# SSD output and z with channels on partitions, roots through memory, half the gate's adaLN moved

## The chip, the cores and the metric

The kernel runs on one core of a Trainium2 chip. The metric is the device time of one execution in microseconds, here the median of three runs. The engines are TensorE (PE, its weight loads PEld), VectorE (DVE), ScalarE (ACT), GpSimd (POOL) and the sync engine (SP), which issues nearly all the DMAs, in program order.

## The reference, cut to what matters

A trunk of two layers on one sequence of L = 256 steps and D = 2048 channels, float32. Layer A is a Mamba-2 SSD mixer, layer B a dilated attention. Each layer gets shift, scale and gate from a conditioning vector c (adaLN), and ends in a residual sum and a LayerNorm. The change lies in layer A:

```python
z, xBC, dt = split(h @ in_w)                 # z: 4096, xs: 4096, B and C: 1024 each, 64 heads
xBC = silu(causal_conv(xBC));  xs, B, C = split(xBC)
dt = softplus(dt + dt_bias);   acum = cumsum(dt * -exp(A_log))
# per group g of 8 (8 heads of 64 channels, one B and C of 128 states), s <= l
y[l] = sum_s (C[l]·B[s]) * exp(acum[l] - acum[s]) * dt[s] * xs[s]   + D_skip * xs[l]
y = y * silu(z)
y = y * rsqrt(mean(y^2 over the group's 512 channels) + eps) * norm_g
out = y @ out_w                              # 4096 -> 2048
x = layer_norm(alpha * x + (1 + gate) * out)
```

## The kernel before, in words

**Products.** Every float32 operand of a large product is split into a high and a low part, and three products are summed: high by high, high by low, low by high. Weights arrive in pieces of 512 KB (`load_piece`, L90, six `raw` buffers); ScalarE makes the high half (`whi`, L100), VectorE the low half (`wlo`, L102), with four buffers of each, so weights can be prepared up to four pieces ahead. A product has one of three forms. `cm_piece` (L151 to 153) holds the weights in TensorE and moves 256 time steps: 24 matmuls of 256 columns a piece, and the result has channels on partitions. `tm_piece` (L232 to 234, in the order of L224 where `low_last` is set) holds the activations and moves 512 weight columns: 12 matmuls of 512 a piece, with time on partitions. `cm_wide` (L190, L193) is a variant of the first.

**Stages.** In the start stage the adaLN dots of shift and scale (L317, one VectorE instruction of 2048 elements for each 128 outputs) make h, while the first pieces of several products run by a table, `order`; 27 of the 64 pieces of z lie here. Then comes a loop over the groups: `product` makes B and C, xs or z of the next group; `scores` (L743) makes C·B; `stage1` (L754) loads the cumulated decays of four heads onto all partitions (`cbc`, L760, two buffers), makes the decay matrix `seg` with Relu and Exp on ScalarE, transposes xs (L776) into `xd`; `stage2` (L793) makes the part of the first half of the sequence (`po`, L798) and the diagonal parts (`py`, L809), adds, multiplies by silu(z), squares (L812) and takes the root (`rsqrt`, L275 to 281, on VectorE); `stage3` (L817) scales y by it on ScalarE (L820), with time on partitions. The last z product (group 7) has the last group's stage1 beside it.

**Out.** `y_tiles` (L857) transposes y (L864) to channels on partitions, multiplies by the norm's weight and splits it: high on ScalarE (L868), low on VectorE (L869). Group 0 is done in the last z product; `y_ahead` does groups 1 to 7 in the first of four out products (n = 0 to 3, `tm_chunk` over `wout[n]`, 16 pieces of two 128-channel tiles each, 512 of the 2048 output channels). Beside n=0 run the second half of the gate's dots (eight), then `gate_out` (a transpose, a copy at L330, a write to `gated`); after each n the gate is broadcast from there and `residual` (L904, L905) is made. V and K, attention and its own out product follow, and are untouched.

**Order.** Each engine runs its instructions in an order that the tile framework's planner sets from the program; `issue_after` pins single ones behind others, and `background(*rate)` takes one job (such as a dot) from a queue every so many pieces.

## Time and profile before

| | us |
|---|---|
| median of three runs (1224.0 to 1226.15) | 1224.74 |
| the profiled execution's own time | 1223.81 |
| its span in the trace, at a clock of 0.999 | 1222.0 |
| TensorE busy | 1208.8 |
| VectorE busy | 1019.6 |
| ScalarE busy | 703.9 |
| start stage and first product, about | 0 to 200 |
| loop over groups, about | 200 to 479 |
| last z product, group 7 | 482.3 to 507.9 |
| first out product, n=0 | 507.9 to 561.4 |

Times in the trace count from the span's first instruction; the profiled execution's own time is 1.8 us longer than the span. In a row of the timeline stand the start, the time it took, the engine, the line, the operation, output and input tiles and their sizes, how many in a row, and in brackets the idle time ahead with what ended it. In a group's row the last columns are busy time in us, mean ns of one, and idle time ahead. A matmul's shown length includes its way through the array, so its price is the distance from its start to the next one's. A float32 matmul of two float32 operands leaves two records.

### The profile page before, as it was taken

How to read it: one execution, taken by the hardware profiler on the slowest of the kernel's cores; microseconds unless marked ns; L12 is line 12 of the kernel's file. 1: busy time of each engine (PE TensorE's matmuls, PEld its weight loads, DVE VectorE, ACT ScalarE, POOL GpSimd, SP SyncE). 2: the span in 40 equal slices, each digit the busy share in tenths (PEclk: the TensorE clock that was granted, in tenths of full speed). 3: DMA queues.
4: the chain of work that ended last, by engine and by line, in shares of the span. 5: the costliest groups of instructions: out<-in, count | busy, mean ns of one | idle time of the engine just before them, and what ended most of it. 6: DMA issues, size and time to landing. Idle time of an engine off the chain costs nothing.

```text
span 1222.0 us, 19072 instructions
## 1 busy us (share of the span) xinstructions
PE 1208.8 (99%) x7244; PEld 1039.5 (85%) x7244; DVE 1019.6 (83%) x1450; ACT 703.9 (58%) x1057; POOL 3.9 (0%) x8
## 2 busy tenths in 40 slices
PE   8999999999999999999999999999999999999998
PEld 8889998898888888788888888888888888888886
DVE  6989997899988999899778588888987885756886
ACT  4554567787698898764335455444435844444751
POOL 0000000000000000000000000000000000000001
PEclk9999999999999999999999999999999999999999
DMA  9999976796765556689998668989997875365673
GB/s 374 421 421 423 422 264 239 259 327 224 230 190 194 182 173 207 226 327 334 370 317 298 211 203 342 350 344 379 385 376 280 281 261 174 113 193 160 193 260 69
DMA packets 81372, 335.94 MB, mean 275 GB/s; under 512 B 9200, under 2 KB 9984, under 8 KB 68480
## 3 DMA queue, kind: packets, MB, share of 16 engines
q1 hardware_dynamic: 80496, 333.59, 75.6%
q0 software_dynamic: 576, 1.05, 0.6%
q8 instruction: 57, 0.93, 0.3%
q14 instruction: 35, 0.29, 0.1%
q10 hardware_dynamic: 208, 0.08, 0.0%
HBM read 331.45 MB, written 3.23 MB: 274 GB/s over the span
## 4 chain that ended last, share of the span: by engine, by line
PE 77%; DVE 13%; ACT 5%; DMA 3%; issue 2%; DVEq 0%; ACTq 0%
PE acc L224 25%; PE acc L190 21%; PE acc L193 11%; DVE wlo L102 4%; DVE araw L317 4%; PE acc L233 3%; PE acc L234 3%; PE acc L232 3%; DMA raw<-in_win 3%; ACT whi L100 2%; DVE cacc L391 2%; PE acc L151 1%; PE acc L153 1%; PE acc L152 1%; PE py L809 1%
## 5 line engine op out<-in xcount | busy, mean ns | idle before, releaser
L100 ACT ACTIVATE whi<-raw 128x1024 fp32r<-128x1024 f32 x389 | 408.2, 1057 | 329.5 <-PE acc L190 107.1
L102 DVE TENSOR_TENSOR wlo<-raw,whi 128x1024 fp32r<-128x1024 f32 x389 | 470.2, 1221 | 128.3 <-ACT whi L100 121.1
L190 PE MATMUL acc<-actT,whi 128*128 128x512 f32 x1280 | 401.7, 394 | 0.5 <-DVE xs L202 0.5
L193 PEld LDWEIGHTS acc<-actT,wlo 128*128 128x128 f32 x1280 | 239.6, 188 | 52.3 <-DVE wlo L102 0.7
L193 PE MATMUL acc<-actT,wlo 128*128 128x256 f32 x1280 | 255.2, 281 | 0.3 <-DVE wlo L102 0.3
L317 DVE SCALAR_TENSOR_TENSOR araw<-araw,cb__72 128x2048 f32<-128x2048 f32 x95 | 217.0, 2284 | 3.2 <-DMA araw<-in_ada 3.0
L190 PEld LDWEIGHTS acc<-actT,whi 128*128 128x128 f32 x1280 | 195.0, 188 | 1.7 <-DVE xs L202 0.9
L224 PE MATMUL acc<-whi,actT 128*128 128x512 f32 x560 | 144.5, 392 | 0.5 <-ACT whi L100 0.5
L224 PEld LDWEIGHTS acc<-whi,actT 128*128 128x128 f32 x560 | 104.2, 188 | 22.0 <-ACT whi L100 0.9
L233 PE MATMUL acc<-wlo,actT 128*128 128x512 f32 x272 | 106.8, 393 | 2.2 <-DVE wlo L102 2.1
L232 PE MATMUL acc<-whi,actT 128*128 128x512 f32 x272 | 105.0, 394 | 0.2 <-ACT sz L664 0.2
L151 PE MATMUL acc<-actT,whi 128*128 128x256 f32 x372 | 103.5, 281 | 1.0 <-ACT sz L664 0.5
L224 PE MATMUL acc<-wlo,actT 128*128 128x512 f32 x384 | 103.6, 391 | 0.0
L153 PE MATMUL acc<-actT,wlo 128*128 128x256 f32 x372 | 101.9, 281 | 1.5 <-DVE wlo L102 1.5
L152 PE MATMUL acc<-actT,whi 128*128 128x256 f32 x372 | 103.0, 279 | 0.0
L234 PE MATMUL acc<-whi,actT 128*128 128x512 f32 x256 | 100.0, 391 | 0.0
L224 PEld LDWEIGHTS acc<-wlo,actT 128*128 128x128 f32 x384 | 71.7, 188 | 14.4
L151 PEld LDWEIGHTS acc<-actT,whi 128*128 128x128 f32 x372 | 69.6, 188 | 2.6 <-ACT sz L664 0.9
L153 PEld LDWEIGHTS acc<-actT,wlo 128*128 128x128 f32 x372 | 68.9, 188 | 2.3 <-DVE wlo L102 2.3
L152 PEld LDWEIGHTS acc<-actT,whi 128*128 128x128 f32 x372 | 70.6, 190 | 0.2
L233 PEld LDWEIGHTS acc<-wlo,actT 128*128 128x128 f32 x272 | 51.1, 188 | 13.8 <-DVE wlo L102 3.7
L232 PEld LDWEIGHTS acc<-whi,actT 128*128 128x128 f32 x272 | 50.9, 188 | 10.5 <-ACT sz L664 0.6
(324 smaller groups left out, 1293.5 us busy)
## 6 DMA issues: line engine op xcount, KB each, us to landing
araw<-in_ada SPq DMA_DIRECT2D x96, 1024.0 KB, 7.3
raw<-in_win SPq DMA_DIRECT2D x109, 512.0 KB, 6.0
raw<-in_wout SPq DMA_DIRECT2D x64, 512.0 KB, 5.7
raw<-in_wbin SPq DMA_DIRECT2D x64, 512.0 KB, 4.1
raw<-in_wxs SPq DMA_DIRECT2D x48, 512.0 KB, 4.5
raw<-in_wv SPq DMA_DIRECT2D x48, 512.0 KB, 6.7
raw<-in_wk SPq DMA_DIRECT2D x48, 512.0 KB, 7.6
cbc<-cumd SPq DMA_DIRECT2D x16, 512.0 KB, 5.1
```

The costliest lines, as they stand in the source:

```text
L100: copied.append(S.activation(hi, raw, AF.Copy))
L102: latest.append(V.tensor_tensor(lo, raw, hi.bitcast(F32), op=ALU.subtract))
L151: T.matmul(o, hi[:, k, c_], ahi[:, kt, :], start=first, stop=False, skip_group_check=True)
L152: T.matmul(o, hi[:, k, c_], alo[:, kt, :], start=False, stop=False, skip_group_check=True)
L153: T.matmul(o, lo[:, k, c_], ahi[:, kt, :], start=False, stop=kt == k1 - 1, skip_group_check=True)
L190: T.matmul(ps[n], hi[:, k, n * P:n * P + P], both(kt), start=kt == 0, stop=False, skip_group_check=True)
L193: T.matmul(ps[n][:, 0, :], lo[:, k, n * P:n * P + P], high(kt), start=False, stop=kt == KT - 1, skip_group_check=True)
L224: T.matmul(ps[b], a_(kt)[:, b * P:b * P + P], w_[:, k, :], start=a_ is ahi and w_ is hi and kt == k0, stop=w_ is lo and kt == k1 - 1)
L232: T.matmul(o, h_, hi[:, k, :], start=kt == k0, stop=False, skip_group_check=part)
L233: T.matmul(o, h_, lo[:, k, :], start=False, stop=False, skip_group_check=part)
L234: end = T.matmul(o, l_, hi[:, k, :], start=False, stop=kt == k1 - 1, skip_group_check=part)
L317: return V.scalar_tensor_tensor(raw, raw, 1.0, cb_, op0=ALU.mult, op1=ALU.mult, accum_out=mod[layer][:, ct, j:j + 1])
```

## The change

Everything between `stage1` and the out product now has channels on partitions. z is made by `cm_quad` (pieces of 24 matmuls of 256 instead of 12 of 512), in the start stage too, so tiles of y and z are [128, 4, 256] instead of [128, 2, 512]. `po` is four matmuls of 128 columns instead of one of 512; `py` is 16 matmuls of 128 columns a group instead of 32 of 64, alternating between the two halves of the output's partitions. The decay factor of `po` is Exp of `cbc`, made in place (`grow`), so `cbc` is read until stage2's product. The D-skip term goes from VectorE to ScalarE. The squares are made in one ScalarE instruction, added over the four channel tiles by two VectorE adds, and over partitions by two matmuls with a column of ones. `stage3` takes the root on VectorE and writes it to memory (`rootd`, GpSimd's queue); `y_tiles` reads it back broadcast over the partitions (sync queue: group 0, groups 1 to 4, groups 5 to 7) and multiplies by norm weight and root in one VectorE instruction a channel tile (L871 in the changed kernel), then splits with one 1024-element instruction on ScalarE (L875) and one on VectorE (L876). The 64 transposes of L864 are gone. `stage3` of group 7 moves into n=0. The second half of the gate's dots goes at one per three pieces over n=0 and n=1, and `gate_out` with the residual of n=0 is made at piece 12 of n=1. Line numbers in the changed kernel differ a little: L760 becomes L752, L224 L228, L317 L320.

The diff, cut to its core:

```diff
-    def cm_quad(src, ahi, alo, rate=(0, 1), k0=0):
+    def cm_quad(src, ahi, alo, rate=(0, 1), k0=0, pre=None):
         ps = acc_pair()
         for q in range(k0 // 2, KT // 2):
+            if pre:
+                pre(q)
             w = first_or(src, q, SHORT)
             if q == KT // 2 - 1:
                 begin_next()
-            cm_piece(src, q, ps, ahi, alo, k0=k0, w=w)
+            end = cm_piece(src, q, ps, ahi, alo, k0=k0, w=w)
             background(*rate)
+        z_end[:] = [end]
...
-        y = [slots.tile([P, 2, 512], F32, name=f"s{g}") for g in range(G)]
+        y = [slots.tile([P, 4, L], F32, name=f"s{g}") for g in range(G)]
...
+        rootd = dr.tile([G * L], F32, name="rootd", bufs=1)
...
+                ps = cm_quad(src, hhi, hlo, rate=R, k0=k0, pre=pre)
                 if kind == "z":
-                    ps = tm_chunk(src, hh_, hl_, rate=R, k0=k0, pre=pre, low_last=False)
                     if g not in sz:
-                        sz[g] = p0.tile([P, 2, 512], F32, name="sz")
+                        sz[g] = p0.tile([P, 4, L], F32, name="sz")
                     with behind_next():
-                        for b in range(2):
+                        for w in range(2):
+                            c_ = slice(2 * w, 2 * w + 2)
                             if part is not None:
-                                V.tensor_tensor(part[:, b, :], ps[b], part[:, b, :], op=ALU.add)
-                            S.activation(sz[g][:, b, :], part[:, b, :] if part is not None else ps[b], AF.Silu)
+                                V.tensor_tensor(part[:, c_, :], ps[w], part[:, c_, :], op=ALU.add)
+                            S.activation(sz[g][:, c_, :], part[:, c_, :] if part is not None else ps[w], AF.Silu)
                     return
...
+                    for n, rows_ in enumerate((slice(0, 64), slice(64, 128))):
+                        S.activation(cbc[rows_, 0:4:2, 0, :], cbc[rows_, n:4:2, 1, :], AF.Exp)
+                    grow.append(cbc[:, 0:4:2, 0, :])
...
-                    V.tensor_tensor(y[g][:, b, :].rearrange("p (h e) -> p h e", h=HPG), heads,
-                                    dskip[:, g * HPG:(g + 1) * HPG, None].to_broadcast([P, HPG, 64]),
-                                    op=ALU.mult)
...
+                for i in range(4):
+                    S.activation(y[g][:, i, :], xs[g][:, i, :], AF.Copy, scale=pv("dsk")[:, 4 * g + i:4 * g + i + 1])
+                return segs, xd, cb, xo, grow
+
+            def stage2(g, segs, xd, cb, xo, grow):
...
                 po = aux.tile([P, 512], F32, name="aux")
-                T.matmul(po, cb[:, 2, :], xo, start=True, stop=True)
-                V.tensor_tensor(xo.rearrange("p (h e) -> p h e", h=HPG), po.rearrange("p (h e) -> p h e", h=HPG),
-                                dec[:, 1, g * HPG:(g + 1) * HPG, None].to_broadcast([P, HPG, 64]), op=ALU.mult)
-                V.tensor_tensor(y[g][:, 1, :], xo, y[g][:, 1, :], op=ALU.add)
-                behind = z_end[-1] if g in (0, 4, 7) else None
+                behind = z_end[-1] if g in (0,3,4,7) else None
+                for i in range(4):
+                    c_ = slice(i * P, i * P + P)
+                    with tc.issue_after(behind.ins) if behind is not None else ExitStack():
+                        behind = T.matmul(po[:, c_], xo[:, c_], cb[:, 2, :], start=True, stop=True)
+                xo = xo.rearrange("p (i n) -> p i n", i=4)
+                for w in range(2):
+                    c_ = slice(2 * w, 2 * w + 2)
+                    V.tensor_tensor(xo[:, c_, :], po.rearrange("p (i n) -> p i n", i=4)[:, c_, :], grow[w], op=ALU.mult)
+                V.tensor_tensor(y[g][:, :, P:], xo, y[g][:, :, P:], op=ALU.add)
+                for w in range(2):
+                    py = aux2.tile([P, 2, L], F32, name="py")
+                    for b in range(2):
+                        for hh in range(4):
+                            h = 4 * w + hh
+                            t_ = slice(64 * (hh % 2), 64 * (hh % 2) + 64)
+                            with tc.issue_after(behind.ins):
+                                behind = T.matmul(py[t_, hh // 2, b * P:b * P + P], xd[:, b, 64 * h:64 * h + 64],
+                                         segs[w][:, hh, b, :], start=True, stop=True)
+                    c_ = slice(2 * w, 2 * w + 2)
+                    V.tensor_tensor(y[g][:, c_, :], py, y[g][:, c_, :], op=ALU.add)
+                V.tensor_tensor(y[g], y[g], sz[g], op=ALU.mult)
+                sq = sz[g]
+                S.activation(sq, y[g], AF.Square)
+                V.tensor_tensor(sq[:, 0:2, :], sq[:, 0:2, :], sq[:, 2:4, :], op=ALU.add)
+                V.tensor_tensor(sq[:, 0, :], sq[:, 0, :], sq[:, 1, :], op=ALU.add)
+                return sq[:, 0, :]
+
+            def stage3(g, sums):
+
+                ss = (aux if g == G - 1 else aux2).tile([P, 512], F32, name="aux" if g == G - 1 else "py")[:, :2]
                 for b in range(2):
-                    py = aux2.tile([P, 512], F32, name="py")
-                    for hh in range(HPG):
-                        e_ = slice(64 * hh, 64 * hh + 64)
-                        for t_ in (slice(0, 64), slice(64, 128)):
-                            with tc.issue_after(behind.ins) if behind is not None else ExitStack():
-                                T.matmul(py[t_, e_], segs[hh // 4][:, hh % 4, b, t_], xd[:, b, e_], start=True, stop=True)
-                    V.tensor_tensor(y[g][:, b, :], py, y[g][:, b, :], op=ALU.add)
-                    V.tensor_tensor(y[g][:, b, :], y[g][:, b, :], sz[g][:, b, :], op=ALU.mult)
-                    S.activation(py, y[g][:, b, :], AF.Square, accum_out=ss[:, b:b + 1])
+                    T.matmul(ss[:, b:b + 1], sums[:, b * P:b * P + P], ones[:, 0:1], start=True, stop=True)
                 ms = sm.tile([P, 2], F32, name="ms")
                 V.tensor_scalar(ms, ss, 1.0 / 512, EPS, op0=ALU.mult, op1=ALU.add)
-                return rsqrt(ms, "a")
-
-            def stage3(g, rs):
-
-                for b in range(2):
-                    S.activation(y[g][:, b, :], y[g][:, b, :], AF.Copy, scale=rs[:, b:b + 1])
+                nc.gpsimd.dma_start(rootd[g * L:g * L + L].rearrange("(b p) -> p b", p=P), rsqrt(ms, "a"))
...
+                if g == 0:
+                    roots[0] = p0.tile([P, L], F32, name="cacc", bufs=3)
+                    bcast(roots[0], rootd)
+                elif g in (1, 5):
+                    t = slots.tile([P, 4, L], F32, name=f"s{g // 5}")
+                    roots.update({g + j: t[:, j, :] for j in range(min(4, G - g))})
+                    bcast(t.rearrange("p i l -> p (i l)")[:, :min(4, G - g) * L], rootd, g * L)
+                rb = roots[g]
                 for i in range(4):
-                    ct = 4 * g + i
-                    if i % 2 == 0:
-                        pt = aux.tile([P, 512], F32, name="aux").rearrange("p (i l) -> p i l", i=2)
-                    for b in range(2):
-                        T.transpose(pt[:, i % 2, b * P:b * P + P], y[g][:, b, i * P:i * P + P], ident)
-                    w = pv("normg")[:, ct:ct + 1]
-                    hi, lo = (t.rearrange("p (r j) -> p r j", r=2) for t in y_to(ct))
-                    by_parity = pt[:, i % 2, :].rearrange("p (j r) -> p r j", r=2)
-                    S.activation(hi, by_parity, AF.Copy, scale=w)
-                    V.scalar_tensor_tensor(lo, by_parity, w, hi.bitcast(F32), op0=ALU.mult, op1=ALU.subtract)
-
+                    V.scalar_tensor_tensor(y[g][:, i, :], y[g][:, i, :], pv("normg")[:, 4 * g + i:4 * g + i + 1], rb,
+                                           op0=ALU.mult, op1=ALU.mult)
+                val = y[g].rearrange("p i (j r) -> p i r j", r=2)
+                hi, lo = (t.rearrange("p i (r j) -> p i r j", r=2) for t in y_to(g))
+                S.activation(hi, val, AF.Copy)
+                V.tensor_tensor(lo, val, hi.bitcast(F32), op=ALU.subtract)
+
+            y_first, roots = [], {}
+
+            def y_to(g):
+                return y_first if g == 0 else (yhi[g // 4][:, 4 * g % 16:4 * g % 16 + 4, :], ylo[g])
...
-            stage3(G - 1, stage2(G - 1, *st1))
+            rs = stage2(G - 1, *st1)
...
+            if q == 1:
+                stage3(G - 1, rs)
             if q % 2 == 0 and q // 2 + 1 < G:
                 y_tiles(q // 2 + 1)
...
-        for n in range(4):
-            ps = tm_chunk(wout[n], lambda kt: y_to(kt)[0], lambda kt: y_to(kt)[1],
-                          nk=2 * KT, rate=(1, 4) if n else (1, 2),
-                          pre={0: y_ahead, 3: first_weights}.get(n), split_end=4 if n == 3 else 0)
-            if n == 0:
-                drain()
-                pin[0] = latest[-3].ins
-                state[0] = 0
-                queue(pn, cols1[:11])
-            if n == 3:
-                drain()
+        spare = {}
+
+        def joined(n, ps):
             if n in (0, 3):
-                spare = (slots.tile([P, 1024], F32, name="s0") if n == 0 else
-                         pn.tile([P, D], F32, name="araw", bufs=2))
...
+
+        def gate_done(q):
+            if q == 12:
+                drain()
+                pin[0] = latest[-3].ins
+                state[0] = 0
+                queue(pn, cols1[:11])
+                joined(0, kept.pop())
+
+        kept = []
+        for n in range(4):
+            ps = tm_chunk(wout[n], lambda kt: y_to(kt // 4)[0][:, kt % 4, :], lambda kt: y_to(kt // 4)[1][:, kt % 4, :],
+                          nk=2 * KT, rate=(1, 3), pre={0: y_ahead, 1: gate_done, 3: first_weights}.get(n),
+                          split_end=4 if n == 3 else 0)
+            if n == 3:
+                drain()
+            if n == 0:
+                kept.append(ps)
+            else:
+                joined(n, ps)
...
-    put("dsk", np.broadcast_to(a_D[0], (P, 64)))
+    put("dsk", np.repeat(a_D[0].reshape(32, 2), 64, axis=1).T)
...
```

How it moves instructions, at three places. First VectorE in n=0, from the end of the root of group 7 (`ay`) on; `ylo` is the low half of y, `prm` holds the norm's weights, `s_6480` the roots of groups 5 to 7. Before:

```order
L281 SCALAR_TENSOR_TENSOR ay<-at,ay 128x2
L869 SCALAR_TENSOR_TENSOR ylo_5570<-aux,prm,actT 128x256
L102 TENSOR_TENSOR wlo<-raw,whi 128x1024
L317 SCALAR_TENSOR_TENSOR araw,mod_80<-araw,cb__72 128x2048
L869 SCALAR_TENSOR_TENSOR ylo_5570<-aux,prm,actT 128x256 x2
```

And changed:

```order
L284 SCALAR_TENSOR_TENSOR ay<-at,ay 128x2
L102 TENSOR_TENSOR wlo<-raw,whi 128x1024
L876 TENSOR_TENSOR ylo_6269<-s_98,actT 128x1024
L102 TENSOR_TENSOR wlo<-raw,whi 128x1024 x2
L320 SCALAR_TENSOR_TENSOR araw,mod_80<-araw,cb__72 128x2048
L871 SCALAR_TENSOR_TENSOR s_99<-s_99,prm,s_6480 128x256 x4
L102 TENSOR_TENSOR wlo<-raw,whi 128x1024
```

The first reader of the roots of groups 5 to 7 now stands three low halves of weights, one of y and a dot behind the root, and a low half of weights follows it directly.

Second the sync queue from the last z pieces (`in_win`) into n=0 (`in_wout`). Before:

```order
L760 DMA cbc<-cumd 128x1024
L90 DMA raw<-in_wxs 128x1024
L90 DMA raw<-in_win 128x1024 x3
L760 DMA cbc<-cumd 128x1024
L90 DMA raw<-in_win 128x1024 x5
L90 DMA raw<-in_wout 128x1024 x8
```

And changed:

```order
L90 DMA raw<-in_win 128x1024 x8
L90 DMA raw<-in_wout 128x1024
L752 DMA cbc<-cumd 128x1024 x2
L63 DMA cacc<-rootd 128x256
L90 DMA raw<-in_wout 128x1024 x4
L63 DMA s_6284<-rootd 128x1024
L90 DMA raw<-in_wout 128x1024 x5
```

Both loads of group 7's decays moved behind all the z pieces and one out piece, and reads of the roots stand among the out pieces.

Third TensorE from group 7's stage2 into n=0. Before:

```order
L798 MATMUL aux<-xo,cb 128x512
L809 MATMUL py<-xd,seg 64x64 x32
L864 MATMUL aux<-cc,s_95 128x128 x4
L224 MATMUL acc<-whi,xs 128x512 x8
L224 MATMUL acc<-wlo,xs 128x512 x4
```

And changed:

```order
L792 MATMUL aux<-cb,xo 128x128 x4
L805 MATMUL py<-seg,xd 64x128 x16
L228 MATMUL acc<-whi,xs 128x512 x8
L228 MATMUL acc<-wlo,xs 128x512 x4
L228 MATMUL acc<-whi,xs 128x512 x8
L228 MATMUL acc<-wlo,xs 128x512 x4
L228 MATMUL acc<-whi,actT 128x512 x4
L820 MATMUL aux<-cc,sz 128x1 x2
```

No transposes stand between the pieces any more; the two sums of group 7 come in the third piece.

62 lines of the change are left out of this document (22 added, 40 removed).

## The prediction

> **What bounds the kernel now.** I read the page's busy line first, then the chain of waits that ended last:
>
> ```profile
> PE 1208.8 (99%) x7244; PEld 1039.5 (85%) x7244; DVE 1019.6 (83%) x1450; ACT 703.9 (58%) x1057; POOL 3.9 (0%) x8
> PE 77%; DVE 13%; ACT 5%; DMA 3%; issue 2%; DVEq 0%; ACTq 0%
> ```
>
> TensorE is busy for 99% of the span and holds 77% of the chain, but VectorE holds 13%: there are places where it ends last. So I asked for the busy times by stage (window, its length, then PE, PEld, DVE, ACT, POOL, the clock, DMA share and GB/s): most of the start stage, the loop over groups, z of group 7, the first out product (n=0) and the second.
>
> ```profile
> 46.00:180.00 134.00, 132.84 (x895) 121.72 (x894) 124.13 (x139) 71.48 (x92) 0.00 (x0) 1.00 0.97 392
> 200.00:479.00 279.00, 277.20 (x1945) 242.16 (x1944) 254.65 (x437) 224.62 (x386) 0.00 (x0) 1.00 0.68 228
> 479.00:507.60 28.60, 27.90 (x185) 22.63 (x184) 26.42 (x50) 23.40 (x44) 0.00 (x0) 1.00 0.43 146
> 507.60:561.20 53.60, 53.60 (x316) 43.38 (x316) 50.80 (x79) 32.07 (x54) 0.00 (x0) 1.00 0.86 316
> 561.20:604.70 43.50, 43.50 (x194) 35.96 (x193) 35.32 (x35) 16.87 (x17) 0.00 (x0) 1.00 1.00 383
> ```
>
> In every stage TensorE comes first. In n=0, where most of the removed transposes lie, VectorE is busy for 50.8 of 53.6 us, so what TensorE loses there beyond about 3 us is no gain unless VectorE loses it too. In n=1 it has 8 us free, which is where half the gate's dots go.
>
> **The transposes.** The group, and four of them standing between products:
>
> ```profile
> L864 PE MATMUL aux<-cc,s 128*128 128x128 f32 x64 | 11.8, 274 | 0.0
> ...
> 495.37 0.79 PE L864 MATMUL aux<-cc,s 128*128 128x128 f32 x4
> 496.86 0.50 PE L233 MATMUL acc<-wlo,actT 128*128 128x512 f32 x1 [0.70 <-DVE wlo L102]
> ...
> 499.25 0.60 PE L864 MATMUL aux<-cc,s 128*128 128x128 f32 x4
> 499.60 0.47 PE L232 MATMUL acc<-whi,actT 128*128 128x512 f32 x1
> ```
>
> Four take 0.35 us, start to start, so 64 take 5.6 us: 8 in z of group 7 (0.7), 56 in n=0 (4.9). At 496.86 stands a wait on weights; it is dealt with below. Removed: -5.6.
>
> **py, po and z.** The rows of the loop: a z piece (24 steps of 512 columns), po and py, a piece of 256 columns (24 steps); then 46 steps of 256 in the start stage; then one 128-column matmul.
>
> ```profile
> 331.44 0.39 PE L232 MATMUL acc<-whi,actT 128*128 128x512 f32 x1
> 336.88 1.02 PE L798 MATMUL aux<-xo,cb 128*128 128x512 f32 x2
> 337.83 2.08 PE L809 MATMUL py<-xd,seg 128*64 128x64 f32 x64
> 339.85 0.38 PE L151 MATMUL acc<-actT,whi 128*128 128x256 f32 x1
> 342.33 0.28 PE L151 MATMUL acc<-actT,whi 128*128 128x256 f32 x1
> 345.05 0.28 PE L151 MATMUL acc<-actT,whi 128*128 128x256 f32 x1
> ...
> 99.09 0.28 PE L151 MATMUL acc<-actT,whi 128*128 128x256 f32 x1
> 104.50 0.28 PE L152 MATMUL acc<-actT,whi 128*128 128x256 f32 x1
> ...
> 479.19 0.27 PE L776 MATMUL aux<-cc,xs 128*128 128x128 f32 x1
> 479.30 1.02 PE L798 MATMUL aux<-xo,cb 128*128 128x512 f32 x2
> ```
>
> A step of 512 is 5.44/24 = 226.7 ns, one of 256 is 2.72/24 = 113.3 ns: exactly half. In the start stage it is 5.41/46 = 117.6 ns, though, 4.3 more. A z piece turns 12 steps of 512 into 24 of 256. The 27 pieces in the start stage then cost 24 x 4.3 ns = 0.10 us each, +2.7 (bounds 0 and 2.7, as the start stage may owe its pace to its full DMA share); the 37 later ones 0 by the loop's rows and +3.7 by the start's, and I take +1.0. The Trainium skill, "TensorE: Matmul & The Clock Gate", section "Wait — 56ns, not 53.3ns?", gives a warm matmul a fixed 2.5 ns beside its columns, which speaks against narrower ones. By it 768 more cost an estimated 1.9 us everywhere alike; the loop's two rows show no such cost, the start's a larger one.
>
> Py takes 337.83 to 339.85, 2.02 us, for 64 records that fill 32 pairs of halves, 0.063 a pair. It becomes 16 pairs of twice the columns: at 0.11 (479.19 to 479.30) 1.76 us, -2.1 over eight groups; by the transposes' 0.088 -4.9, by a quarter of po's 0.475 (0.119) -1.0. I take -2.1. Po keeps its columns and its 0.95.
>
> The new sums are two matmuls a group, four records, between 0.063 and 0.11 each: 1.9 to 3.5, taken as +2.4.
>
> TensorE's own work: -5.6 - 2.1 + 2.4 + 2.7 + 1.0 = -1.6.
>
> **ScalarE and VectorE in the loop.** ScalarE gains four D-skip copies and four half-sized exponentials and loses the scaling by the root: some 1.6 us a group, 14 in all, on 224.6 of 279: hidden in its 54 free us. VectorE loses the D-skip product there and gains two adds: even. Both hide behind TensorE's 277.2.
>
> **z of group 7.** The decay rows (cbc) now stay held until stage2 of the group before has read them, and the last load waits for that.
>
> ```profile
> 465.74 0.33 SPq L760 DMA_DIRECT2D cbc<-cumd  x1
> ...
> 482.27 0.50 PE L232 MATMUL acc<-whi,actT 128*128 128x512 f32 x1
> ...
> 482.11 2.15 ACT L765 ACTIVATE seg<-cbc,cumT 128x128 f32<-128x128 f32 x7
> 485.18 1.28 ACT L767 ACT_TABLE_LOAD   x1
> 491.96 1.05 ACT L767 ACTIVATE seg<-seg 128x1024 f32<-128x1024 f32 x1
> ...
> cbc<-cumd SPq DMA_DIRECT2D x16, 512.0 KB, 5.1
> ```
>
> So far the last load is issued 16.5 us before z7 starts (482.27), and ScalarE begins at once. Now it can be issued about 1.3 us before the start and lands 5.1 later, at +3.8. What stands on ScalarE from there to the weight copy of piece 5 is sixteen Relus (0.307 each), two big exponentials (0.95), small ones, two table loads (1.28) and three weight copies (0.95), which puts that copy at +15.7; TensorE asks for it at +15.3. VectorE's low half (1.14) follows: a stall of 1.5 (0 to 4). It takes the place of what z7 idles now: the stage lasts 25.6 us (482.27 to 507.87), of which its matmuls fill 23.9 (eight pieces of 2.72, the transposes, group 7's scores). 1.5 for 1.7: -0.2.
>
> **The first out product.** Its ends, the last z weight half ahead of it, and VectorE's prices there:
>
> ```profile
> 507.87 1.02 PE L798 MATMUL aux<-xo,cb 128*128 128x512 f32 x2
> 561.42 0.48 PE L224 MATMUL acc<-whi,xs 128*128 128x512 f32 x1
> ...
> 506.49 1.23 DVE L102 TENSOR_TENSOR wlo<-raw,whi 128x1024 fp32r<-128x1024 f32 x1 [1.49 <-ACT whi L100]
> 509.65 0.69 DVE L801 TENSOR_TENSOR s<-xo,s 128x512 f32<-128x512 f32 x1
> 510.26 0.69 DVE L810 TENSOR_TENSOR s<-py,s 128x512 f32<-128x512 f32 x1
> 535.20 2.35 DVE L102 TENSOR_TENSOR wlo<-raw,whi 128x1024 fp32r<-128x1024 f32 x2
> 537.47 0.87 DVE L869 SCALAR_TENSOR_TENSOR ylo<-aux,prm,actT 128x256 fp32r<-128x256 f32 x2
> 538.26 2.28 DVE L317 SCALAR_TENSOR_TENSOR araw<-araw,cb__72 128x2048 f32<-128x2048 f32 x1
> 553.84 1.22 DVE L102 TENSOR_TENSOR wlo<-raw,whi 128x1024 fp32r<-128x1024 f32 x1
> ```
>
> It lasts 53.55 us: po and py 2.97, 16 pieces of 2.72 (43.5), the transposes 4.9, and 2.2 of small waits and restarts. TensorE alone would now need 2.7 + 43.5 + 0.3 of sums = 46.5.
>
> VectorE's queue, from the low half ahead of it (which ends at 507.72, 0.1 before the stage) to the low half of piece 14 (now the row at 553.84): start to start a low half or any 1024 operation costs 1.14 (535.20 to 537.47), a product of 256 0.40, a 512 operation 0.61, a dot 2.2 (538.26, with its read). There: 28 products by norm and root 11.2, seven low halves of y 8.0, twelve of weights 13.7, four dots (seven before) 8.8, group 7's stage2 4.7, its root 0.9: 47.3, ending 47.1 after the start. Then come the last third of piece 14 (0.9) and piece 15 (2.72): the end at +50.7, 4.2 later than TensorE alone. Against before, the three dots gone (-6.6) have paid for the low halves of y, which were part of the 28 products.
>
> In front of the products of groups 5 to 7 stands the root's way through memory: VectorE to GpSimd's queue, to memory, and back by the sync queue.
>
> ```profile
> out<-u POOLq DMA_DIRECT2D x4, 256.0 KB, 8.1
> s<-gated SPq DMA_DIRECT2D x3, 256.0 KB, 8.6
> gated<-row SPq DMA_DIRECT2D x2, 8.0 KB, 2.5
> ```
>
> The order puts group 7's root about 22.8 after the start and its first reader at 29.6, so 6.8 us are free. For the write the rows give 2.5 (8 KB, sync queue) to 8.1 (256 KB, GpSimd), for the broadcast back 5.1 (cbc's) to 8.6: 7.6 to 16.7 together. The root has 1 KB, so I stay near the low end at 7.8: a wait of 1.0. Behind it on VectorE stand the weights' low halves, so TensorE pays it. By the Trainium skill, "DMA: Bandwidth & Descriptors", section "Anatomy of one DMA — SWDGE (gpsimd) path", a GpSimd DMA costs about 2.0 us fixed, most of it the receipt of the write; with cbc's 5.1 the way would be an estimated 7.1, the wait 0.3. No run here shows a small GpSimd write.
>
> n=0: +4.2 + 1.0 - 2.2 = +3.0 of waits, beside the work counted above.
>
> **The gate's second half and the residual.** The rest of the dots go into n=1's 8 free us. The residual of n=0 is now made in n=1, ahead of piece 12: row to memory 2.5, broadcast up to 8.6, two products 1.2, a copy 0.3 are 12.6 us, while pieces 12 to 15 and the one that weights run ahead give 13.6 until n=2 needs the accumulators: 0. With that cover gone it would cost what exceeds 13.6.
>
> **Sum:** -1.6 - 0.2 + 3.0 = +1.2 on the profiled execution's 1223.8 gives 1225.0; the median lies 0.9 above that execution, so **1226 us**: no change that a measurement of this kernel can tell (within 0.2%, 1222.3 to 1227.2). Its own range, from py, z, the stall of z7 and the way of the root, is 1222 to 1229.
>
> **Rivals.** *VectorE does not bind n=0* (faster): weights' halves are made far enough ahead, or the new operations are cheaper from on-chip memory than from the accumulators. Then TensorE's work and the waits removed count: 1224.7 - 1.6 - 1.7 - 2.2 = **1219**. For it: low halves run up to four pieces ahead. Against it: VectorE's 50.8 of 53.6.
> *The root's way is long* (slower): from 6.8 us on each microsecond is paid in n=0, by VectorE standing at the first product of group 5. At 12 to 16 us, which the 8.1 and 8.6 rows allow, 4 to 8 more than I took: **1230 to 1234**. For it: the two rows, and weight transfers at a DMA share of 0.86. Against: they moved 256 KB.
> *The late cbc binds z7* (slower): 3 us more of stall, **1229**.
> *The halves of py don't overlap* across alternate outputs: 32 steps of 0.11 are 3.5 us for 2.02, +1.5 in eight groups where I had -0.26: **1240**. Against: the present halves do overlap.
>
> **Chances.** Forecast 0.45, VectorE not binding 0.23, long root 0.20, late cbc 0.08, no overlap 0.04. A quarter of the forecast's own cases lie below 1222.3 or above 1227.2, some on each side: faster 0.30, same 0.37, slower 0.33. The range of 8 in 10 takes in the fast rival and most of the long root: 1217 to 1233.
>
> **What would show it.** py's records of a group within 1.8 us; z pieces in the start stage at 2.82 us and later ones at 2.72; n=0 lasting 50.7 to 51.7 us, with TensorE waiting there on VectorE's weights and VectorE waiting for a DMA of the roots at its products; ScalarE waiting for cbc in z7. Wrong would be: n=0 at 46 to 48 us with no such waits, or VectorE standing at the products for more than 3 us.

## The result

The changed kernel takes 1276.24 us, median of five runs (1275.24 to 1278.53), against 1224.0 beside it (five runs): a ratio of 1.0426, 95% interval 1.0411 to 1.0442. It is 52 us slower. The forecast was 1226 us with a range to 1233, so both the number and the range were wrong.

The page of the changed kernel, its busy line and its chain of waits:

```profile
PE 1224.1 (96%) x7772; PEld 1082.2 (85%) x7772; DVE 1027.0 (81%) x1458; ACT 715.1 (56%) x1058; POOL 9.7 (1%) x16
PE 58%; DVE 18%; DMA 12%; ACT 8%; issue 4%; SPq 0%; DVEq 0%; ACTq 0%
```

TensorE's busy time grew by only 15 us, but its share of the chain fell from 77 to 58%; DMA's rose from 3 to 12%, VectorE's from 13 to 18%. More of the time now goes into waiting for transfers and for VectorE. The busy times by stage, cut where TensorE begins the first po, the last z product's po, group 7's po and n=1 (columns as in the prediction):

```profile
245.90:519.00 273.10, 249.75 (x1779) 225.97 (x1778) 219.58 (x379) 203.76 (x356) 3.79 (x5) 0.97 0.63 191
519.00:550.15 31.15, 28.18 (x250) 26.91 (x250) 28.04 (x62) 26.41 (x48) 1.45 (x2) 1.00 0.75 165
550.15:611.27 61.12, 52.61 (x238) 42.10 (x237) 53.17 (x81) 26.93 (x27) 0.72 (x1) 0.89 0.77 264
```

The loop in the kernel before, cut at the same places:

```profile
240.70:479.30 238.60, 237.78 (x1693) 206.89 (x1693) 223.85 (x392) 194.38 (x339) 0.00 (x0) 1.00 0.67 222
```

In the loop TensorE, whose busy time before filled it to within 1 us, now stands idle for 23 us, and in n=0, which it filled wholly, for 8.5; the granted clock is 0.97 and 0.89 there. Stage by stage, with two of the experiments below, in us of the profiled executions:

| | before | changed | own tile for the decay | and root by matmul |
|---|---|---|---|---|
| start to the first po | 240.7 | 245.9 | 246.1 | 246.5 |
| loop, to the last z product's po | 238.6 | 273.1 | 246.5 | 243.7 |
| last z product | 28.6 | 31.2 | 32.4 | 32.1 |
| po of group 7 and n=0 | 53.6 | 61.1 | 64.3 | 52.8 |
| n=1 | 43.6 | 44.1 | 44.1 | 44.1 |
| the rest | 616.9 | 618.2 | 618.9 | 618.8 |
| span | 1222.0 | 1273.6 | 1252.3 | 1238.0 |

So 34.5 of the 51.6 us are lost in the loop, where the forecast saw nothing, 7.6 in n=0 and 5.2 in the start.

**Where the loop's time goes.** Groups 2 and 3 in the timeline, TensorE, VectorE, the sync queue and ScalarE one after another:

```profile
324.49 0.38 PE L792 MATMUL aux<-cb,xo 128*128 128x128 f32 x2
...
336.75 0.76 DVE L796 TENSOR_TENSOR xo<-aux,cbc 128x256 f32<-128x256 f32 x2
...
337.26 0.73 SPq L752 DMA_DIRECT2D cbc<-cumd  x1
...
343.34 1.06 ACT L100 ACTIVATE whi<-raw 128x1024 fp32r<-128x1024 f32 x1 [5.17 <-DMA raw<-in_win]
349.48 0.99 ACT L757 ACTIVATE seg<-cbc,cumT 128x128 f32<-128x128 f32 x3 [5.07 <-DMA cbc<-cumd]
```

Group 2's po is there at 324.49, but VectorE comes to the product that reads cbc only at 336.75, behind convolutions and weight halves in its queue. Only then can the sync queue load the next group's decays into that buffer (337.26), and they land 12.2 us later, when ScalarE has stood at its first Relu for 5 us. Behind that Relu stand weight copies, behind the load on the sync queue stand weight pieces, so TensorE runs dry. The same happens in later groups. What waited for what, in the whole span (total us, times, longest):

```profile
ACT seg L757 <- DMA cbc<-cumd: 32.2, 7, 10.3
PE acc L153 <- DVE wlo L102: 11.8, 10, 3.7
PE acc L197 <- DVE wlo L102: 11.4, 6, 4.6
```

And the DMA groups that matter here, with their KB and median landing; cbc's was 5.1 before:

```profile
cbc<-cumd SPq DMA_DIRECT2D x16, 512.0 KB, 10.4
...
rootd<-ay POOLq DMA_DIRECT2D x8, 1.0 KB, 9.1
gated<-row SPq DMA_DIRECT2D x2, 8.0 KB, 1.4
```

In the kernel before, ScalarE waited 1.0 us for cbc in all:

```profile
ACT seg L765 <- DMA cbc<-cumd: 1.0, 1, 1.0
```

**Where n=0's goes.** The way of group 7's root, on VectorE, GpSimd, the sync queue, ScalarE and TensorE:

```profile
572.22 0.16 DVE L284 SCALAR_TENSOR_TENSOR ay<-at,ay 128x2 f32<-128x2 f32 x1
...
574.08 0.72 POOL L823 DMA_DIRECT2D rootd<-ay  x1 [25.89 <-DMA raw<-in_wout]
...
571.87 0.33 SPq L313 DMA_DIRECT2D araw<-in_ada  x1
582.58 0.33 SPq L63 DMA_DIRECT2D s<-rootd  x1
...
587.76 0.48 DVE L871 SCALAR_TENSOR_TENSOR s<-s,prm,s 128x256 f32<-128x256 f32 x1 [6.82 <-DMA s<-rootd]
...
589.07 1.06 ACT L100 ACTIVATE whi<-raw 128x1024 fp32r<-128x1024 f32 x1 [9.35 <-DMA raw<-in_wout]
...
590.62 2.08 PE L228 MATMUL acc<-wlo,actT 128*128 128x512 f32 x4 [6.56 <-DVE wlo L102]
...
597.04 1.07 PE L228 MATMUL acc<-whi,actT 128*128 128x512 f32 x4
```

The root is ready at 572.4 (22.2 after the stage's start; 22.8 was forecast), its write is issued at 574.08, the read follows at 582.58, and VectorE has it at 587.76: 15.4 us for which 7.8 were allowed. VectorE asked at 580.9 (30.8 after the start, forecast 29.6). In the meantime the sync queue, which waits in order, issued nothing between 571.87 and 582.58, weights included; ScalarE waited 9.35 us for them. And the matmuls after the stall are slow: 16 of them from 590.62 to 597.04, 6.4 us where 3.6 are normal.

### The profile page after: what moved, and what is told of

It reads as the page before. It is cut to its first block, busy times and chain, and to the rows that moved or that the text cites. A ratio compares the mean times of both kernels' runs of the same rounds, so it can differ in the third digit from the quotient of the medians.

```text
span 1273.6 us, 20143 instructions
## 1 busy us (share of the span) xinstructions
PE 1224.1 (96%) x7772; PEld 1082.2 (85%) x7772; DVE 1027.0 (81%) x1458; ACT 715.1 (56%) x1058; POOL 9.7 (1%) x16
## 4 chain that ended last, share of the span: by engine, by line
PE 58%; DVE 18%; DMA 12%; ACT 8%; issue 4%; SPq 0%; DVEq 0%; ACTq 0%
PE acc L228 21%; PE acc L194 17%; PE acc L197 9%; DVE wlo L102 5%; DMA cbc<-cumd 4%; DVE araw L320 4%; DVE cacc L392 3%; DMA raw<-in_win 3%; ACT whi L100 3%; ACT seg L757 2%; DMA araw<-in_ada 2%; PE acc L153 1%; DMA raw<-in_wout 1%; PE acc L151 1%; PE acc L152 1%
## 5 line engine op out<-in xcount | busy, mean ns | idle before, releaser
L197 PEld LDWEIGHTS acc<-actT,wlo 128*128 128x128 f32 x1280 | 241.8, 190 | 66.7 <-DVE wlo L102 14.2
L197 PE MATMUL acc<-actT,wlo 128*128 128x256 f32 x1280 | 258.1, 283 | 11.4 <-DVE wlo L102 11.4
L153 PE MATMUL acc<-actT,wlo 128*128 128x256 f32 x884 | 242.5, 280 | 11.8 <-DVE wlo L102 11.8
L151 PE MATMUL acc<-actT,whi 128*128 128x256 f32 x884 | 245.8, 280 | 1.8 <-ACT whi L100 0.7
L152 PE MATMUL acc<-actT,whi 128*128 128x256 f32 x884 | 244.5, 278 | 0.0
L320 DVE SCALAR_TENSOR_TENSOR araw<-araw,cb__72 128x2048 f32<-128x2048 f32 x95 | 217.3, 2287 | 2.1 <-DMA araw<-in_ada 1.7
L194 PEld LDWEIGHTS acc<-actT,whi 128*128 128x128 f32 x1280 | 197.6, 190 | 7.5 <-ACT whi L100 3.5
L153 PEld LDWEIGHTS acc<-actT,wlo 128*128 128x128 f32 x884 | 164.7, 189 | 14.7 <-DVE wlo L102 14.4
L151 PEld LDWEIGHTS acc<-actT,whi 128*128 128x128 f32 x884 | 166.9, 189 | 3.9 <-ACT whi L100 1.3
L152 PEld LDWEIGHTS acc<-actT,whi 128*128 128x128 f32 x884 | 167.1, 189 | 0.0
L228 PE MATMUL acc<-whi,actT 128*128 128x512 f32 x560 | 144.5, 392 | 0.5 <-ACT whi L100 0.5
L228 PEld LDWEIGHTS acc<-whi,actT 128*128 128x128 f32 x560 | 105.3, 189 | 23.1 <-ACT whi L100 0.9
L228 PE MATMUL acc<-wlo,actT 128*128 128x512 f32 x384 | 105.4, 397 | 6.8 <-DVE wlo L102 6.8
L228 PEld LDWEIGHTS acc<-wlo,actT 128*128 128x128 f32 x384 | 73.3, 191 | 23.7 <-DVE wlo L102 7.6
L228 PE MATMUL acc<-whi,ylo 128*128 128x512 f32 x208 | 58.0, 402 | 0.9 <-DVE ylo L876 0.9
L757 ACT ACTIVATE seg<-cbc,cumT 128x128 f32<-128x128 f32 x128 | 40.6, 390 | 32.3 <-DMA cbc<-cumd 32.2
L228 PEld LDWEIGHTS acc<-whi,ylo 128*128 128x128 f32 x208 | 39.9, 192 | 9.7 <-DVE ylo L876 0.9
## 6 DMA issues: line engine op xcount, KB each, us to landing
cbc<-cumd SPq DMA_DIRECT2D x16, 512.0 KB, 10.4
```

What stands on the lines that cost most here:

```text
L151: T.matmul(o, hi[:, k, c_], ahi[:, kt, :], start=first, stop=False, skip_group_check=True)
L152: T.matmul(o, hi[:, k, c_], alo[:, kt, :], start=False, stop=False, skip_group_check=True)
L153: end = T.matmul(o, lo[:, k, c_], ahi[:, kt, :], start=False, stop=kt == k1 - 1, skip_group_check=True)
L194: T.matmul(ps[n], hi[:, k, n * P:n * P + P], both(kt), start=kt == 0, stop=False, skip_group_check=True)
L197: T.matmul(ps[n][:, 0, :], lo[:, k, n * P:n * P + P], high(kt), start=False, stop=kt == KT - 1, skip_group_check=True)
L228: T.matmul(ps[b], a_(kt)[:, b * P:b * P + P], w_[:, k, :], start=a_ is ahi and w_ is hi and kt == k0, stop=w_ is lo and kt == k1 - 1)
```

## The experiments

Comparisons are with the kernel before, run beside them. "n=0" is from group 7's po to n=1.

**1. A tile of its own for the decay factor.**

```diff
+                    gw = px.tile([P, 2, P], F32, name="gw", bufs=4)
-                        S.activation(cbc[rows_, 0:4:2, 0, :], cbc[rows_, n:4:2, 1, :], AF.Exp)
-                    grow.append(cbc[:, 0:4:2, 0, :])
+                        S.activation(gw[rows_], cbc[rows_, n:4:2, 1, :], AF.Exp)
+                    grow.append(gw)
```

> The changed kernel, but the decay factor of po (grow) has a tile of its own (four buffers), so that cbc is free after ScalarE's exponentials as it was before the change. Theory H (held decay rows: the load of cbc waits for stage2's product, ScalarE stands at its Relus with weight copies behind them, TensorE starves): the loop from the first po to the last z product falls from 273 us back to 238 to 242 and that z product from 31 to 27 to 29, so the time is about 1240 us (1235 to 1246), with the stall in the first out product still there. Rival L (the loop is slow because ScalarE and VectorE have more to do, or z has narrower matmuls): no more than 5 us are won, 1271 or above.

Measured: 1250.16 us (ratio 1.0206, 1.0183 to 1.0229). The loop and the last z product:

```profile
246.10:492.60 246.50, 242.77 (x1794) 223.37 (x1792) 220.77 (x386) 222.45 (x374) 3.80 (x5) 0.99 0.71 214
492.60:525.00 32.40, 28.42 (x232) 27.54 (x233) 30.16 (x64) 25.41 (x42) 1.45 (x2) 0.89 0.78 135
```

What ScalarE still waits for at the Relus:

```profile
ACT seg L757 <- DMA cbc<-cumd: 2.7, 1, 2.7
ACT gw L762 <- DMA cbc<-cumd: 3.9, 2, 3.8
```

26.6 us of the loop come back with one tile of 1 KB per partition (in four buffers), half of all that was lost. The held buffer is shown as the main cause, the rival L has fallen. But the loop is still 7.9 longer than before, and the last z product has not gained at all, so the expectation was 10 us too hopeful: something else sits there. One candidate, which no run tried by itself: ScalarE is busy for 222.5 us of this loop, 28 more than before and 19 more than in the changed kernel, and most of that is loads of its function tables, 1.28 us each. 33 of them stand in the loop, for 16 before and 18 in the changed kernel, because Exp and Silu alternate more often with the new order.

**2. The hold alone, in the kernel before.**

```diff
-                V.tensor_tensor(xo.rearrange(...), po.rearrange(...), dec[:, 1, ...].to_broadcast([P, HPG, 64]), op=ALU.mult)
+                for w in range(2):
+                    c_ = slice(256 * w, 256 * w + 256)
+                    V.tensor_tensor(xo[:, c_].rearrange("p (i n) -> p i n", i=2),
+                                    po[:, c_].rearrange("p (i n) -> p i n", i=2), hold[w][:, 0:4:2, 0, :], op=ALU.mult)
```

> The kernel before, with one part of the change alone: stage2's product of po is made in two instructions that read cbc in place of the decay column, so cbc is held until then; nothing else differs (y gets a wrong factor). Theory H: the loop gets 20 to 37 us longer, 1245 to 1262 us. Rival L: holding costs nothing, 1224 to 1228.

Measured: 1239.39 us (1.0112, 1.0097 to 1.0128): 15 us, of which 11.6 in the loop (250.2 for 238.6). ScalarE waits for cbc as often as in the changed kernel, for half the time:

```profile
ACT seg L765 <- DMA cbc<-cumd: 16.3, 7, 5.6
```

Holding costs much by itself, so the mechanism is confirmed from the other side, below the expected 20. Put in alone it costs 15, taken out of the changed kernel it gives 26: there ScalarE has more to do, which may be why. How the other 11 divide was not separated.

**3. z with 256 columns alone, in the kernel before.**

```diff
-                    ps = tm_chunk(src, hh_, hl_, rate=R, k0=k0, pre=pre, low_last=False)
+                    ps = [t.rearrange("p a l -> p (a l)") for t in cm_quad(src, hhi, hlo, rate=R, k0=k0, pre=pre)]
...
-                        tm_piece(source[k], q, pss[k], hh_, hl_, k0=k0, k1=k1, w=halves[i])
+                        cm_piece(source[k], q, pss[k], hhi, hlo, k0=k0, k1=k1, w=halves[i], ...)
```

> The kernel before, with z's pieces made by the 24 matmuls of 256 columns and all else as it was (its z then lies in another layout than the rest assumes, so y is wrong). The prediction's term: 27 pieces in the start stage at 0.10 us and 37 later at 0 to 0.10, +3.7 (2.7 to 6.4): 1228.4 us. Rival (the start stage is paced by its transfers, not by the matmuls): 0 to 1 us, 1224.7 to 1225.7.

Measured: 1227.98 us (1.0030, 1.0020 to 1.0040), +3.5 us: the forecast term was +3.7. In its profile the first po comes at 243.2 for 240.7 (+2.5). The Trainium skill's fixed 2.5 ns a matmul ("TensorE: Matmul & The Clock Gate", "Wait — 56ns, not 53.3ns?") would have given an estimated 1.9. The row of the start stage was the better price.

**4. The root written by the sync queue.**

```diff
-                nc.gpsimd.dma_start(rootd[...], rsqrt(ms, "a"))
+                (nc.sync if g == G - 1 else nc.gpsimd).dma_start(rootd[...], rsqrt(ms, "a"))
```

> The changed kernel, but the root of group 7 is written to memory by the sync queue and not by GpSimd's. Theory R (the root's way through memory, 574.1 to 587.7, stops VectorE and holds the weight loads behind the read on the sync queue): the write lands in 2 to 3 us for 8.5, the stall of 6.6 us and the slow matmuls behind it go, n=0 falls from 61 us to 50 to 53, the time to 1266 us (1264 to 1270). Rival (VectorE's own load sets the length of n=0): it stays at 58 or more, 1273 to 1277.

Measured: 1277.25 us (1.0434, 1.0411 to 1.0456), nothing won; n=0 62.6 us. Its sync queue and VectorE:

```profile
567.95 0.38 SPq L823 DMA_DIRECT2D rootd<-ay  x1
577.93 0.33 SPq L63 DMA_DIRECT2D s<-rootd  x1
585.02 2.86 DVE L871 SCALAR_TENSOR_TENSOR s<-s,prm,s 128x256 f32<-128x256 f32 x7 [6.84 <-DMA s<-rootd]
```

From the write to the read that waits for it are 10.0 us on this queue too. That GpSimd's queue is the slow part has fallen.

**5. The root by a matmul, on top of experiment 1.**

```diff
+                for b in range(2):
+                    V.tensor_scalar(dg[:, b * P:b * P + P], ident, rs_[:, b:b + 1], None, op0=ALU.mult)
+                T.matmul(rp, ones, dg, start=True, stop=True)
+                roots[g] = rp
```

This is done for group 7 alone; the roots of groups 5 and 6 are read from memory together.

> The decay factor in its own tile, and the root of group 7 not through memory: two VectorE products of 128 columns put it on a diagonal, one matmul by ones spreads it over the partitions, and VectorE reads it from there; the read of the roots of groups 5 and 6 waits for nothing late. Theory R2 (whatever queue writes the root, it lands only when the loads issued before it have drained, 8 to 10 us, and the read that waits in order on the sync queue holds the weight loads): the stall of 10 us in n=0 goes, po to the end of n=0 falls from 64 us to 50 to 54, the time from 1250 to 1239 (1236 to 1243). Rival (VectorE alone sets n=0 at about 60): 1247 or more.

Measured: 1241.69 us (1.0138, 1.0123 to 1.0153), as expected. The loop, the last z product and n=0:

```profile
246.50:490.20 243.70, 241.33 (x1795) 222.12 (x1793) 220.71 (x386) 222.76 (x374) 3.80 (x5) 1.00 0.70 216
490.20:522.30 32.10, 28.02 (x232) 27.10 (x233) 29.32 (x63) 25.38 (x42) 1.45 (x2) 0.89 0.76 136
522.30:575.10 52.80, 49.91 (x240) 40.58 (x239) 51.16 (x76) 26.89 (x27) 0.00 (x0) 0.97 0.80 273
```

n=0 falls from 64.3 to 52.8 us. With the root there in time it lasts about what the prediction's VectorE queue gave (50.7), and VectorE is busy for 51.2 of it. That the two agree so well is in part luck: 8 of the 28 products by the root, which the prediction counted in n=0, are done ahead of it in this run, and five dots end in it where four were counted. TensorE also waits there, with the new sums of group 7 for their squares:

```profile
PE aux L821 <- DVE sz L814: 2.0, 1, 2.0
```

That wait is not what is left above 50.7: in experiment 8, where these sums stand two pieces later, it is 0.4 us and n=0 still lasts 53.2.

**6. The gate's part undone, on top of 5**: the loop over n, its rates, the residual and `gate_out` as in the kernel before.

```diff
-        for n in range(4):
-            ps = tm_chunk(wout[n], ..., rate=(1, 3), pre={0: y_ahead, 1: gate_done, 3: first_weights}.get(n), ...)
+            ps = tm_chunk(wout[n], ..., rate=(1, 4) if n else (1, 2), pre={0: y_ahead, 3: first_weights}.get(n), ...)
```

> As the run with the root by a matmul, but the gate's second half, gate_out and the residual of n=0 are back where they were before the change (a dot every two pieces in n=0, one job every four pieces in n=1 to 3). The prediction (VectorE sets the length of n=0, three dots are 6.6 us there): n=0 grows by 4 to 7 us, the time by 3 to 6, 1242 to 1245. Rival (n=0 has room on VectorE once the root is there in time): within 1.5 us of that run.

Measured: 1246.54 us (1.0179, 1.0162 to 1.0195), 4.9 more; n=0 is 60.2 for 52.8 us, with a wait on weights that was not there:

```profile
565.67 2.07 PE L228 MATMUL acc<-wlo,actT 128*128 128x512 f32 x4 [2.97 <-DVE wlo L102]
```

So this part of the change is a gain, and of about the size of the dots it moves (6.6). VectorE does bind n=0.

**7. The D-skip term back from ScalarE to VectorE, on top of 5.**

```diff
-                for i in range(4):
-                    S.activation(y[g][:, i, :], xs[g][:, i, :], AF.Copy, scale=pv("dsk")[:, 4 * g + i:4 * g + i + 1])
...
+                    for i in (2 * w, 2 * w + 1):
+                        V.scalar_tensor_tensor(y[g][:, i, :], xs[g][:, i, :], pv("dsk")[...], py[:, i % 2, :],
+                                               op0=ALU.mult, op1=ALU.add)
```

> As the run before it, and the D-skip term moved from ScalarE (four copies a group) into VectorE's add of py (four 256-element instructions for two of 512). Theory A (ScalarE's extra work is not hidden: it delays weight copies at single places, in the first group, group 5 and the last z product): 3 to 8 us are won, 1231 to 1236. Rival, which the prediction held (ScalarE's work is hidden in its free time): no more than 1.5 us either way, 1237 to 1241.

Measured: 1246.83 us (1.0184, 1.0167 to 1.0202), 5 more, a miss for both. The last z product gains 1.8 us (30.3), as if ScalarE's work were not free there, but the loop (247.2) and n=0 (58.6) lose 3.5 and 5.8. Why was not taken apart. The loop differs by 2.8 us even between experiments 1, 5, 10 and 11, whose loops are the same (246.5, 243.7, 243.9 and 244.8); here ScalarE was busy in it for 18 us less than in run 5 but waited 11.2 us for cbc, for 3.9 there. In n=0 the D-skip work itself is only about 0.4 us more for VectorE, at the prediction's prices. But the read of the roots of groups 1 to 4 was issued at 528.97 for 511.40 in run 5, so that all 28 products by the root lie in n=0, where 20 did. So the run does not show that VectorE's time is worth more than ScalarE's.

**8. The sums of group 6 later, on top of 5.** In the last z product two waits followed one another, in run 5:

```profile
503.18 0.58 PE L821 MATMUL py<-cc,sz 128*128 128x1 f32 x4 [1.77 <-DVE sz L814]
505.98 0.58 PE L151 MATMUL acc<-actT,whi 128*128 128x256 f32 x1 [2.22 <-ACT whi L100]
```

```diff
-                if q == 2:
-                    stage3(G - 2, rs)
+                if q == 5:
+                    stage3(G - 2, rs)
```

The two matmuls are also pinned behind the last one of the piece before, and `stage3` of group 7 stands two pieces later in n=0 (`q == 3` for `q == 1`).

> The run with the root by a matmul, and the two sums of group 6, which stand in the last z product behind its second piece, are held until behind its fifth. Theory P (a small matmul at the head of TensorE's queue waits for squares and adds that are not made yet, 1.9 us, and the piece behind it then waits 2.4 for weights): that product falls from 32.2 us to 28 to 29 and the time from 1241.7 to 1238 (1236.5 to 1239.5). Rival (both waits are for ScalarE, which has more to do there, and only move): within 1.5 us of 1241.7.

Measured: 1240.26 us (1.0137, 1.0119 to 1.0155), 1.4 below run 5 with overlapping intervals; the product stays at 33 us. The wait on weights has moved and grown:

```profile
504.87 0.58 PE L153 MATMUL acc<-actT,whi 128*128 128x256 f32 x1 [4.52 <-ACT whi L100]
```

Theory P has fallen, the rival holds: the last z product waits for ScalarE. There stand, between the weight copies at 491.0 and 503.8, two sets of eight Relus (2.15 and more), two exponentials, the square (1.05), the D-skip copies (0.45 each) and two table loads (1.28). These 12.7 us are longer than the four pieces made ahead last (4 x 2.72).

**9. The write's price by itself**: columns written to memory that nobody reads, in the kernel before.

```diff
+                nc.gpsimd.dma_start(probe[g * L:g * L + L].rearrange("(b p) -> p b", p=P), rs_)
...
+                (nc.sync if b else nc.gpsimd).dma_start(probe2[8 * hq + 2 * i + b], den)
```

> The kernel before with small writes added that nobody reads: each group's root (1 KB) to memory from GpSimd's queue, in the loop and in n=0, and in the attention sixteen columns of 512 B, half from GpSimd's queue and half from the sync queue. It measures the disputed cost by itself. Theory Q (a small write lands behind the loads that are under way): 8 to 10 us in the loop and in n=0, 2 to 5 us in the attention, where the DMA share is about 0.5, on both queues. Theory F (a fixed price of GpSimd's queue): 8 to 10 us everywhere on that queue, 1.5 to 3 on the sync queue. The time stays within 3 us of the kernel before.

Measured, issue to landing:

```profile
probe<-ay POOLq DMA_DIRECT2D x8, 1.0 KB, 9.4
probe<-den POOLq DMA_DIRECT2D x8, 0.5 KB, 9.2
probe<-den SPq DMA_DIRECT2D x8, 0.5 KB, 9.9
```

Neither theory: it is 9 to 10 us on both queues and in both places. That the time would stay was a miss: 1244.04 us (1.0164, 1.009 to 1.0237), 20 more. The loop is unchanged (239.1), but n=0 grew to 59.9 us, for a reason that was not traced, and in the attention ScalarE's next sums go to the column that a write is still reading:

```profile
ACT sc L1174 <- DMA probe<-den: 18.5, 5, 5.3
```

**10. The root as rows, on top of 1**: a transpose and a copy to [2, 128], then the same GpSimd write.

```diff
+                T.transpose(pt, rs_, ident)
+                V.tensor_copy(rr, pt)
+                nc.gpsimd.dma_start(rootd[g * L:g * L + L].rearrange("(b p) -> b p", p=P), rr)
```

> The changed kernel with the decay factor in its own tile, and the root of group 7 still through memory by GpSimd's queue, but as two rows of 512 B (a transpose and a copy ahead of it) in place of a column of 4-byte elements over 128 partitions. The probes showed 9.2 to 9.9 us for columns on both queues, in the loop and in the attention alike, and 2.6 for the gate's rows. Theory C (the price is that of a column of single elements): the write lands in 2 to 4 us, the read is issued 5 us earlier, po to the end of n=0 falls from 64 us to 55 to 60 and the time from 1250 to 1242 to 1246. Rival (the write waits for the loads ahead of it, whatever its form): still 8 us or more, the time within 2 us of 1250.

Measured: 1252.22 us (1.0230, 1.0213 to 1.0247). The write of the two rows landed sooner than the columns of the other groups in the same execution (median of seven, and the one):

```profile
rootd<-ay POOLq DMA_DIRECT2D x7, 1.0 KB, 8.9
rootd<-rr POOLq DMA_DIRECT2D x1, 1.0 KB, 5.0
```

By this one write about 4 of the 9 us belong to the column form; the rest was not taken apart. Yet the time did not follow, n=0 is 64.6 us. The root's last step, the copy of the rows and the read:

```profile
550.69 0.16 DVE L284 SCALAR_TENSOR_TENSOR ay<-at,ay 128x2 f32<-128x2 f32 x1
...
554.49 0.27 DVE L831 COPY rr<-aux 2x128 f32<-2x128 f32 x1
...
560.16 0.33 SPq L63 DMA_DIRECT2D s<-rootd  x1
```

The copy came on VectorE only 3.6 us after the root, behind a dot, and took back what the write had won: the read went out 38.1 us after group 7's po, for 37.5 in experiment 1. So the way as a whole did not get shorter, and the run does not decide whether the stall hangs on the write.

**11. The read split, on top of 1**: roots of groups 5 and 6 in one read, that of group 7 in its own.

```diff
-                    bcast(t.rearrange("p i l -> p (i l)")[:, :min(4, G - g) * L], rootd, g * L)
+                    bcast(t.rearrange("p i l -> p (i l)")[:, :(4 if g == 1 else 2) * L], rootd, g * L)
+                elif g == G - 1:
+                    bcast(roots[g], rootd, g * L)
```

> The changed kernel with the decay factor in its own tile; all roots go through memory as in the change, but the last read is split: the roots of groups 5 and 6 are read when they are there, and that of group 7 by a read of its own later. Theory G (what stops n=0 is that one read serves groups 5 to 7 and so makes group 5 wait for the root of group 7; the way itself, 8 to 10 us for the write, is hidden by two groups' products): po to the end of n=0 falls from 64 us to 53 to 56, the time from 1250 to 1239 to 1243, as with the matmul. Rival (the read in order on the sync queue holds the weight loads while it waits, whoever needs it): 60 us or more remain, 1247 or above.

Measured: 1245.62 us (1.0175, 1.0138 to 1.0211), between the two; n=0 57.0 us. VectorE hardly waits for roots any more, but ScalarE still waits 6.59 us for weights that stand behind the read on the sync queue (at 564.07), and TensorE stalls once:

```profile
562.72 1.67 DVE L874 SCALAR_TENSOR_TENSOR s<-s,prm,s 128x256 f32<-128x256 f32 x4 [0.82 <-DMA s<-rootd]
572.23 1.25 PE L228 MATMUL acc<-whi,actT 128*128 128x512 f32 x4 [2.67 <-ACT actT L878]
```

Of the 11.5 us between experiments 1 and 5 in n=0, 7.3 hang on one read that serves three groups and so lets group 5 wait for group 7, and 4.2 on there being a late read at all, by one profiled execution of each (the times of this run spread from 1242.8 to 1251.4).

## Why the prediction was wrong, step by step

- **"Both hide behind TensorE's 277.2" (the loop)** is the step that failed. The change's hold of cbc was priced for the last z product alone; in each of the other groups it is the same load behind the same kind of instruction. It cost 26.6 us there (experiment 1; 28 to 29 by experiments 5, 10 and 11, which have the same loop). The working added up instructions by engine and compared sums with free time; it did not ask, for the buffer that is held longer, when VectorE's queue reaches the releasing instruction (12.3 us after po in group 2), and what stands behind the load and the Relu.
- **The last z product**: a stall of 1.5 was forecast for 1.7 that goes; it grew by 2.6. The mechanism was a late ScalarE, as forecast, but freeing cbc did not shorten it (experiment 1), so the late load was not its cause alone: ScalarE's queue is full there (experiment 8). The clock adds to it: in experiment 1 the granted clock of this stage is 0.89, which takes up to 3.5 of its 32.4 us, for 1.00 in the changed kernel.
- **The root's way**: 7.8 us were taken from a range of 7.6 to 16.7; it is 15.4. The rival with its long way (12 to 16 us, deciding from 6.8 on) described the mechanism and came true beside the loop's loss. Its price was 5 to 9 us, with the 1.0 already in the sum. n=0 lasted 10.4 more than 50.7 (61.1), and 8.3 more than with the root by a matmul (experiment 5). In that is what the rival did not name: the read also holds the weight loads behind it, and the stall slows what follows. The Trainium skill's 2.0 us for a GpSimd DMA ("DMA: Bandwidth & Descriptors", "Anatomy of one DMA — SWDGE (gpsimd) path") does not agree with the trace: 9.1 for 1 KB.
- **n=0 without that**: 50.7 forecast, 52.8 measured (experiment 5), close in part by luck, since the queue held other items than those added up. The rival "VectorE does not bind n=0" has fallen (experiment 6).
- **z**: +3.7 forecast, +3.5 measured alone (experiment 3). **The gate's move**: the three dots' 6.6 forecast for n=0, 7.4 measured there (experiment 6).
- **py**: 1.76 us a group forecast, 1.89 measured in place of 2.02; the rival without overlap of the halves has fallen:

```profile
551.14 1.97 PE L805 MATMUL py<-seg,xd 128*64 128x128 f32 x32
553.03 2.11 PE L228 MATMUL acc<-whi,xs 128*128 128x512 f32 x8
```

- **The start stage** lost 5.2, about 2.5 of it z (experiment 3). One stall at 233.66 is 2.7 longer than before (3.67 us on a weight half for 0.98), and the half pace behind it takes 1.3 more; together that is more than 5.2, so these parts overlap or something else got shorter. Ahead of it VectorE, which makes that weight half, waits 2.75 us (at 223.97) for group 0's decays from ScalarE; which of ScalarE's new instructions is to blame was not tried.

With experiments 1 and 5 the sum still stands 17 us above the kernel before. Of the 16 us between the two spans 5.8 lie in the start, 5.1 in the loop, 3.5 in the last z product and 1.9 behind n=1. For the last no step was expected and no cause is known; the loop's rest stays open too. No version tried is faster than the kernel before.

## What to carry to other kernels

When a change lets a buffer be read by a later instruction, price it in every iteration: find in the trace when the releasing engine's queue reaches that instruction, then what stands in order behind the next load (on the queue that issues it) and behind its first reader. An engine with a fifth of its time free is not free at the place where it runs full; sums by stage don't show it. A value that is needed on all partitions soon should not go through memory, and a read that serves several users is as late as the latest of its sources.
